# Neighbourhood attention of layer 1: score tiles issued one by one, with the value products of two tiles after every second tile

## The chip, the cores and the metric

The kernel runs on one core of one Trainium2 chip. The metric is the device time of one execution in microseconds (us). The kernel before takes 3551.81 us, the median of 3 runs (3551.78 to 3552.18). One further execution was profiled. Its own time is 3547.52 us, and 3545.7 us lie between its first and its last instruction (the span).

## What is computed

The program has two layers over 2048 latent tokens (a grid of 32 rows by 64 columns) and 256 context tokens, all in float32. The change touches the attention of the second layer ("layer 1") alone. Cut to that:

```python
def one_row(args):                       # one row of 64 queries
    qr, r = args
    r_start = jnp.clip(r - kr // 2, 0, rows - kr)
    kb = lax.dynamic_slice_in_dim(kg, r_start, kr, axis=1)        # 8 rows of keys
    vb = lax.dynamic_slice_in_dim(vg, r_start, kr, axis=1)
    s_lat = jnp.einsum('bqhd,brkhd->bhqrk', qr, kb) * scale + bias
    s_lat = jnp.where(col_mask, s_lat, -jnp.inf)                  # 16 columns of keys
    s_ctx = jnp.einsum('bqhd,bchd->bhqc', qr, k_ctx) * scale
    p = jax.nn.softmax(jnp.concatenate([s_lat, s_ctx], axis=-1), axis=-1)
    return p[..., :kr * GRID_W] @ vb + p[..., kr * GRID_W:] @ v_ctx
...
y = jnp.dot(o * jax.nn.silu(z_x), w_out)
x = x + gate * y
```

There are 16 heads of width 64. Each latent query sees a window of 8 by 16 latent keys and all 256 context keys.

## The kernel before

**Pairs and tiles.** `odd_attention` takes the heads in eight pairs (`j` from 0 to 7). Scores are made transposed: keys on the partitions, queries along the free axis, the two heads of a pair in the two halves of one tile. A *score tile* is 128 keys against all the queries that can see them. A pair has 24 of them: 16 latent ones (l0 to l15, `rect` gives their queries) and 8 context ones (for each of the four blocks of 512 queries, c0 to c3, two halves `u` of the 256 context keys).

**One score tile.** TensorE makes it with eight matmuls on half-arrays (L1785: high times high, low times high, high times low, minus the maximum, each for two heads). It lands in a PSUM buffer `st`; there are two of these, so a tile can begin only when the tile two before it has been read out. ScalarE reads a context tile straight away (`exp`, L108). A latent tile first gets its position bias added by VectorE in one to six pieces (L1961, `st` plus `tab` into `opt`), which is what frees its `st` buffer, and ScalarE then takes `exp` in place.

**Value products.** TensorE multiplies the finished `opt` by the values into PSUM accumulators `o`, one for each block of 512 queries (`tail_ctx` L1797 for context, `tail` L1815 for latent tiles). GpSimd adds the `opt` tiles up into `oacc` (L1821), from which the softmax's denominators come; the two halves of a context block are added first (`sum_ctx`, L1806: c0 and c2 on VectorE, c1 and c3 on GpSimd).

**Ending blocks.** When all tiles of some blocks are done, `finish_blocks` makes the denominators. It is a generator in three parts. The first makes eight matmuls into an `st` buffer (L1840) and a copy on ScalarE; the second takes `Ln`; the third takes `Exp`, then on VectorE L1849 (correction), L1851 (times the gate), L1854 and L1855 (one of each for a block: scale the accumulator, which is then free), and stores the result to `RT1` (L1856). In pairs 0 to 6 the blocks end as [0, 1] and [2, 3], for the last pair as [0], [1] and [2, 3].

**What sets the order.** The order is written out by hand in `steps`: c0 l0 c1 l1 l2 l3 c2 l4 l5 l6 l7 c3 l8 ... l15, twenty steps, where a context step makes both of its tiles. Each step issues its scores, its reading out, then one part of a pending `finish_blocks` (`end`), and puts its value products in the list `pend`. When `pend` holds five steps, `flush(2)` issues the value products of the two oldest; a block that is complete then gets the first part of its ending there. So TensorE sees value products after every second step, and between them two to four score tiles. The loads of the next pair hang on the step number `s` (L1929 to L1941), and on the last pair so do the weights of the output projection (`out_w`, `split` with L1299 on VectorE). The projection of the first 128 tokens (`first`, L131 to L133) begins inside the last pair's steps l14 and l15, in an `o` buffer that block 0 must have given up.

A pool of eleven buffers `opt` holds the tiles that wait for their value products.

Of the kernel before, what the change touches and what calls it, by code (L numbers as in the profile page):

```python
# [12 lines left out]
AF = mybir.ActivationFunctionType  # L13
# [4 lines left out]
P = 128  # L18
# [70 lines left out]
class Kern:  # L89
# [1630 lines left out]
    def odd_attention(self, out, pools, left, wout):  # L1720

        nc = self.nc
        self.RT1 = self.scr("RT1", (KD, P, SEQ), F32)
        NR, NC = (len(b) for b in BLOCKS["k"])
        with ExitStack() as es:
            self.ln_exp(self.last_tanh, es)
            gp, rp, fp, ep, mp, pad, *sets, lp = pools
            pp = self.pool(es, "oaPS", bufs=2, space=PSUM, reuse_waits="tile")
            steps = [("l", n) for n in range(16)]
            for n, at in enumerate((0, 2, 6, 11)):  # L1730
                steps.insert(at, ("c", n))
            both = lambda: self.tl(pp, [P, 2, 512], "st", bufs=2)
            halves = []

# [45 lines left out]
            def scores(ps, ks, qs, j):  # L1780
                terms = [(K[j][0], Q[j][0]), (K[j][1], Q[j][0]), (K[j][0], Q[j][1]), (None, M[j % 2])]
                for n, (k, q) in enumerate(terms):
                    for i in range(2):
                        s = slice(i * 64, i * 64 + 64)
                        mm = nc.tensor.matmul(ps(i), ones[s] if k is None else k[s, ks], qs(q[s]), start=n == 0, stop=n == 3)  # L1785
                return mm
# [2 lines left out]

                return [acc[bb // 2][:, i].rearrange("p r c -> p (r c)")[:, (bb % 2) * 512 : (bb % 2) * 512 + n * 512] for i in range(2)]  # L1790

            def tail_ctx(n, pts, j, V, O, acc):
                O[n] = self.tl(pp, [P, 8, 64], "o", bufs=4)
                o = O[n][:].rearrange("p r c -> p (r c)")
                for u in range(2):
                    for i in range(2):
                        mm = nc.tensor.matmul(o[i * 64 : i * 64 + 64, :], V[:, u, i * 64 : i * 64 + 64], pts[u][:, i, :],  # L1797
                                              start=u == 0, stop=False, skip_group_check=True)
                return mm

            def sum_ctx(n, pts, acc):
# [3 lines left out]
                a = acc[n // 2][:].rearrange("p i r c -> p i (r c)")[:, :, (n % 2) * 512 : (n % 2) * 512 + 512]  # L1805
                (nc.gpsimd if n % 2 else nc.vector).tensor_tensor(out=a, in0=pts[0][:], in1=pts[1][:], op=ALU.add)  # L1806

            def tail(n, pts, j, V, O, acc):
                g, c = divmod(n, 4)
                (r0, nr), (c0, w) = rect("k", g, c)  # L1810
                done = {7: [0], 11: [1], 15: [2, 3]}.get(n, [])
                for bb in range(r0 // 8, (r0 + nr - 1) // 8 + 1):
                    a0, a1 = max(r0, bb * 8), min(r0 + nr, bb * 8 + 8)
                    for i in range(2):
                        mm = nc.tensor.matmul(O[bb][i * 64 : i * 64 + 64, a0 - bb * 8 : a1 - bb * 8, c0 : c0 + w],  # L1815
                                              V[:, NCT + n, i * 64 : i * 64 + 64], pts[:, i, a0 - r0 : a1 - r0, :],
                                              start=False, stop=bb in done, skip_group_check=True)
                for hf in range(r0 // 16, (r0 + nr - 1) // 16 + 1):
                    a0, a1 = max(r0, hf * 16), min(r0 + nr, hf * 16 + 16)
                    a = acc[hf][:, :, a0 - hf * 16 : a1 - hf * 16, c0 : c0 + w]  # L1820
                    nc.gpsimd.tensor_tensor(out=a, in0=a, in1=pts[:, :, a0 - r0 : a1 - r0, :], op=ALU.add)  # L1821
# [65 lines left out]
            Q, K, V, Z, tabs, raw = {}, {}, {}, {}, {}, {}  # L1887
# [9 lines left out]
                fill(K[0], ksrc, CTX + g * 512, CTX + g * 512 + 512)  # L1897
            out_w, out_s = weights(), split()
            pend, late, ends, OA, first_sums = [], [], [], {}, {}
            FIRST_SUMS = {1: 0, 3: 1, 8: 2, 12: 3}  # L1900
            all_k, most, last = slice(0, KD), slice(0, KD - 1), slice(KD - 1, KD)

            def flush(n):

                mm = None
                for f, *a in pend[:n]:
                    mm = f(*a)
                del pend[:n]
                for x in late:
                    x[0] -= 1  # L1910
                for x in [x for x in late if x[0] <= 0]:
                    late.remove(x)
                    ends.append(finish_blocks(*x[1:]))
                    mm = next(ends[-1])
                return mm

            def end(after):
# [4 lines left out]

            for j in range(8):
                OA[j] = {}, {}
                for s, (kind, n) in enumerate(steps):
                    g, c = divmod(n, 4)
                    if s in (1, 10) and j + s > 1:
                        gates(*((j - 1, 1) if s == 1 else (j, 0)))
# [12 lines left out]
                    elif s % 2 and s < 16:  # L1941
                        next(out_w)
                    if kind == "c":
                        pts = []
                        for u in range(2):
                            ps, qs = both(), slice(n * 512, n * 512 + 512)
                            mm = scores(lambda i: ps[:, i, :], slice(u * P, u * P + P), lambda q: q[:, qs], j)
                            pts.append(exps())
                            ex = self.act(pts[u][:], ps[:], AF.Exp)
                        first_sums[n] = pts  # L1950
                    else:
                        (r0_, nr), (c0, w) = rect("k", g, c)
                        a, m, d = even(c0, w)
                        ps, pts = both(), exps()[:, :, : nr * w]
                        pt = pts.rearrange("p i (r c) -> p i r c", r=nr)
                        ps = ps[:, :, : nr * m].rearrange("p i (r c) -> p i r c", r=nr)
                        mm = scores(lambda i: ps[:, i], slice(CTX + n * P, CTX + n * P + P),
                                    lambda q: q.rearrange("d (r c) -> d r c", r=32)[:, r0_ : r0_ + nr, a : a + m], j)
                        for ro, ri, rn in pieces("k", 0, g, r0_, nr):
                            for co, ci, cn in pieces("k", 1, c, c0, w):  # L1960
                                bias = nc.vector.tensor_tensor(out=pt[:, :, ro : ro + rn, co : co + cn],  # L1961
                                                               in0=ps[:, :, ro : ro + rn, d + co : d + co + cn],
                                                               in1=tabs[j][:, :, ri : ri + rn, ci : ci + cn], op=ALU.add)
                        ex = self.act(pts, pts, AF.Exp)
                        pts = pt
                    if s in FIRST_SUMS:
                        with self.tc.issue_after(bias.ins):
                            sum_ctx(FIRST_SUMS[s], first_sums[FIRST_SUMS[s]], OA[j][1])
                    pend.insert(len(pend) - ((kind, n) == ("c", 1)), (tail_ctx if kind == "c" else tail, n, pts, j, V[j], *OA[j]))
# [254 lines left out]
```

## Time and profile before

| what | value |
|---|---|
| median of 3 runs | 3551.81 us |
| profiled execution, its own time | 3547.52 us |
| its span | 3545.7 us |
| mean granted TensorE clock | 0.992 |
| layer 1 attention, first score matmul | at 2962.0 us |
| last pair's first score matmul | at 3302.8 us |
| TensorE busy in the whole span | 3432.9 us (97%) |
| VectorE, ScalarE, GpSimd busy | 2406.5, 1459.8, 1037.6 us |

A row of the timeline gives the start in us, the time until the last of the merged instructions ended, engine, line, operation, the tile written and the tiles read, how many instructions were merged, and in brackets how long the engine had been idle before and what released it. PE is TensorE, PEld its weight loads, DVE VectorE, ACT ScalarE, POOL GpSimd, SP the queue that issues most loads. The count of the value products and of the denominators is twice what the program holds, since each runs as two passes. The granted clock (PEclk) is what share of TensorE's full clock the throttle let through in a stretch.

### The profile page before, as it was taken

The page shows a single profiled execution, that of the slowest core. Times are in us where ns is not written, and L with a number is a line of the kernel's source. Part 1 is how long each engine was busy: PE and PEld are TensorE (multiplying, and loading weights), DVE is VectorE, ACT ScalarE, POOL GpSimd, SP SyncE. Part 2 cuts the span into 40 slices and gives each one's busy share as a digit, 9 for nine tenths or more (in the row PEclk, how much of TensorE's full clock was granted, in tenths as well). Part 3 has the DMA queues.
Part 4 walks back from the last instruction along what each step waited for, and adds up shares of the span by engine and source line. Part 5 has one row for each costly group of instructions (what it writes and reads, how often), then busy time and mean ns, then how long its engine had stood idle before and what let it go on. Part 6 is the DMA issues. An engine that isn't in the chain of part 4 may idle for free.

```text
span 3545.7 us, 54709 instructions
## 1 busy us (share of the span) xinstructions
PE 3432.9 (97%) x20228; PEld 2657.4 (75%) x20228; DVE 2406.5 (68%) x4494; ACT 1459.8 (41%) x2570; POOL 1037.6 (29%) x1281
## 2 busy tenths in 40 slices
PE   8999998999999999999999999999999999988799
PEld 6898987888896666665557878888888886555477
DVE  4677755888886777768876654545678883555765
ACT  5445552111114455446664354445422224555532
POOL 1333431111111333322211133333111114666611
PEclk9999999999999999999999999999999999999999
DMA  7555555233325242334525765445755445554374
GB/s 253 147 157 158 151 142 152 92 109 94 95 73 167 67 130 80 111 112 131 175 80 144 144 197 160 136 129 182 242 151 164 152 139 186 199 200 172 111 191 63
DMA packets 349888, 508.40 MB, mean 143 GB/s; under 512 B 32443, under 2 KB 232843, under 8 KB 342661
## 3 DMA queue, kind: packets, MB, share of 16 engines
q1 hardware_dynamic: 297364, 386.91, 35.9%
q0 software_dynamic: 29232, 82.14, 8.8%
q10 hardware_dynamic: 23024, 35.85, 3.0%
q8 instruction: 160, 2.62, 0.3%
q14 instruction: 108, 0.88, 0.1%
HBM read 325.99 MB, written 196.60 MB: 147 GB/s over the span
## 4 chain that ended last, share of the span: by engine, by line
PE 80%; DVE 6%; DMA 5%; ACT 4%; POOL 3%; issue 3%; SPq 0%; ACTq 0%; DVEq 0%; POOLq 0%
PE st L1175 10%; PE gm L133 10%; PE gm L131 10%; PE gm L132 10%; PE av L1085 7%; PE mx L705 4%; PE st L1785 2%; PE o L1364 2%; PE pu L1364 2%; ACT opt L108 2%; PE st L1364 1%; PE pj L1364 1%; POOL oacc L1821 1%; PE o L1815 1%; PE mx L1697 1%
## 5 line engine op out<-in xcount | busy, mean ns | idle before, releaser
L706 DVE TENSOR_REDUCE mm<-mx 128x1 f32<-128x512 f32 (+1 forms) x656 | 389.1, 627 | 84.3 <-PE mx L705 77.1
L108 ACT ACTIVATE apt<-st 128x1024 f32<-128x1024 f32 (+1 forms) x296 | 300.0, 1014 | 304.4 <-PE st L1175 285.0
L1182 DVE TENSOR_TENSOR acc<-acc,apt 128x1024 f32<-128x1024 f32 x256 | 340.6, 1330 | 83.5 <-ACT apt L108 64.9
L1175 PE MATMUL st<-aq,akh 64*128 64x512 f32 x1728 | 311.8, 408 | 1.1 <-ACT apt L108 0.7
L1085 PE MATMUL av<-apt,av 128*64 128x512 f32 x1152 | 265.8, 598 | 0.0
L1821 POOL TENSOR_TENSOR oacc<-oacc,opt 128x528 f32<-128x528 f32 (+4 forms) x192 | 225.4, 1197 | 75.8 <-ACT opt L108 72.8
L705 PE MATMUL mx<-mk,mq 96*128 96x512 f32 (+1 forms) x656 | 236.0, 373 | 7.5 <-DMA mq<-QC 6.7
L1175 PE MATMUL st<-aq,akl 64*128 64x512 f32 (+1 forms) x1152 | 230.2, 391 | 0.0
L108 ACT ACTIVATE u<-gm 128x352 f32<-128x352 f32 (+1 forms) x140 | 68.6, 496 | 374.7 <-PE gm L133 204.5
L1961 DVE TENSOR_TENSOR opt<-st,tab 128x496 f32<-128x496 f32 (+16 forms) x288 | 123.6, 484 | 137.7 <-PE st L1785 132.2
L1175 PEld LDWEIGHTS st<-aq,akh 64*128 64x128 f32 x1728 | 152.6, 185 | 82.9 <-ACT apt L108 28.5
L1703 DVE CUSTOM_DVE_ANT_1 mx<-mx,mtab 128x105 f32<-128x105 f32 (+14 forms) x576 | 182.9, 339 | 46.9 <-PE mx L1697 35.2
L1085 PEld LDWEIGHTS av<-apt,av 128*64 128x64 f32 x1152 | 76.3, 136 | 135.2 <-issue 133.9
L108 ACT ACTIVATE opt<-opt 128x930 f32<-128x930 f32 (+8 forms) x130 | 104.1, 805 | 137.0 <-DVE opt L1961 116.9
L705 PEld LDWEIGHTS mx<-mk,mq 96*128 96x128 f32 x656 | 121.6, 189 | 19.8 <-issue 7.1
L1175 PEld LDWEIGHTS st<-aq,akl 64*128 64x128 f32 (+1 forms) x1152 | 111.7, 184 | 23.7
L1785 PE MATMUL st<-qh,kh 64*128 64x512 f32 (+6 forms) x384 | 83.0, 427 | 42.4 <-ACT opt L108 24.1
L220 POOL TENSOR_TENSOR oss<-oss,mhalf 128x8 f32<-128x8 f32 x68 | 112.2, 1650 | 5.4
L131 PE MATMUL gm<-w1h,hhi 128*128 128x512 f32 x280 | 111.9, 400 | 0.2 <-ACT ovz L108 0.2
L1552 DVE TENSOR_TENSOR onat<-gm,oss 128x512 f32<-128x512 f32 x68 | 46.8, 689 | 95.6 <-POOL oss L220 95.6
L133 PE MATMUL gm<-w1h,hlo 128*128 128x512 f32 x280 | 110.0, 393 | 0.0
L131 PE MATMUL gm<-w0h,hhi 128*128 128x512 f32 x272 | 109.6, 403 | 0.0
(777 smaller groups left out, 9578.3 us busy)
## 6 DMA issues: line engine op xcount, KB each, us to landing
H<-x ACTq DMA_DIRECT2D x32, 512.0 KB
adaw<-ada_w SPq DMA_DIRECT2D x64, 256.0 KB
wraw<-w_od SPq DMA_DIRECT2D x64, 256.0 KB
K1t<-okt POOLq DMA_DIRECT2D x16, 1024.0 KB, 6.6
x<-H SPq DMA_DIRECT2D x31, 512.0 KB
mtab<-rpb_q SPq DMA_DIRECT2D x16, 899.0 KB
x<-xin SPq DMA_DIRECT2D x18, 512.0 KB
x<-xin POOLq DMA_DIRECT2D x18, 512.0 KB, 5.3
```

The costliest lines, as they stand in the source:

```text
L108: return self.nc.scalar.activation(out, in_, func, **kw)
L131: self.nc.tensor.matmul(out, lh(k), rh(k), start=start and j == 0, stop=False)
L132: self.nc.tensor.matmul(out, lh(k), rl(k), start=False, stop=False)
L133: yield self.nc.tensor.matmul(out, ll(k), rh(k), start=False, stop=stop and j == n - 1)
L705: mm = nc.tensor.matmul(ps[:, :w], q[:A_QK, (t % 6) * P : (t % 6) * P + P], k[:A_QK, k0 : k0 + w], start=True, stop=True)
L706: nc.vector.tensor_reduce(out=m[:, t, n : n + 1], in_=ps[:, :w], axis=AX.X, op=ALU.max)
L1085: mm = nc.tensor.matmul(O[j, nb][i * 64 : i * 64 + 64, :w], V[j, kt // TT][:, kt % TT, i * 64 : i * 64 + 64], pts[:, i, :w], start=n == 0, ...
L1175: mm = nc.tensor.matmul(ps[:, o // 64, :w], k[o : o + r, kb, kq], Q[o : o + r, qb, :w], start=m == 0, stop=m == 4)
L1182: added = nc.vector.tensor_tensor(out=acc[:, :, :w], in0=a[:, :, :w], in1=pts[:, :, :w], op=ALU.add)
L1364: self.mm = self.nc.tensor.matmul(ps, x[:, k, :], y, start=start and k == 0 and n == 0, stop=k == self.H4 - 1 and n == 2, skip_group_check ...
L1703: nc.vector.tensor_tensor_reduce(out=s, in0=s, in1=tb[:, ri : ri + rn, ci : ci + cn], scale=1.0, scalar=-3e38, op0=ALU.add, op1=ALU.max, a ...
L1821: nc.gpsimd.tensor_tensor(out=a, in0=a, in1=pts[:, :, a0 - r0 : a1 - r0, :], op=ALU.add)
```

## The change

The order is now by score tiles: `units` has 24 entries, (kind, n, u), and a context block takes two neighbouring ones. Each unit issues one tile, one part of a pending ending, and puts the value products of that one tile in `pend`; `flush(2)` still comes when `pend` holds five. So two score tiles stand between any two groups of value products. The step numbers on which the sums of context halves hang are moved so that they stay at the same latent tiles (l0, l1, l5, l8). The numbers on which loads hang are kept, so they come after fewer tiles than before. The last pair's ending of block 0 is run through in one go where its first part is issued.

```diff
-            steps = [("l", n) for n in range(16)]
-            for n, at in enumerate((0, 2, 6, 11)):
-                steps.insert(at, ("c", n))
+            units = [("l", n, 0) for n in range(16)]
+            for n, at in enumerate((0, 3, 8, 14)):
+                units[at:at] = [("c", n, u) for u in range(2)]
...
-            def tail_ctx(n, pts, j, V, O, acc):
-                O[n] = self.tl(pp, [P, 8, 64], "o", bufs=4)
+            def tail_ctx(n, pts, j, V, O, acc, u):
+                if u == 0:
+                    O[n] = self.tl(pp, [P, 8, 64], "o", bufs=4)
                 o = O[n][:].rearrange("p r c -> p (r c)")
-                for u in range(2):
-                    for i in range(2):
-                        mm = nc.tensor.matmul(o[i * 64 : i * 64 + 64, :], V[:, u, i * 64 : i * 64 + 64], pts[u][:, i, :],
-                                              start=u == 0, stop=False, skip_group_check=True)
+                for i in range(2):
+                    mm = nc.tensor.matmul(o[i * 64 : i * 64 + 64, :], V[:, u, i * 64 : i * 64 + 64], pts[:, i, :],
+                                          start=u == 0, stop=False, skip_group_check=True)
...
-            FIRST_SUMS = {1: 0, 3: 1, 8: 2, 12: 3}
+            FIRST_SUMS = {2: 0, 5: 1, 11: 2, 16: 3}
...
                     ends.append(finish_blocks(*x[1:]))
                     mm = next(ends[-1])
+                    if x[1] == [0]:
+                        for _ in ends.pop():
+                            pass
...
-                for s, (kind, n) in enumerate(steps):
+                for s, (kind, n, u) in enumerate(units):
...
                     if kind == "c":
-                        pts = []
-                        for u in range(2):
-                            ps, qs = both(), slice(n * 512, n * 512 + 512)
-                            mm = scores(lambda i: ps[:, i, :], slice(u * P, u * P + P), lambda q: q[:, qs], j)
-                            pts.append(exps())
-                            ex = self.act(pts[u][:], ps[:], AF.Exp)
-                        first_sums[n] = pts
+                        ps, pts, qs = both(), exps(), slice(n * 512, n * 512 + 512)
+                        mm = scores(lambda i: ps[:, i, :], slice(u * P, u * P + P), lambda q: q[:, qs], j)
+                        ex = self.act(pts[:], ps[:], AF.Exp)
+                        first_sums[n, u] = pts
...
-                    if j == 7 and 3 < s < 17:
+                    if j == 7 and 3 < s < 20:
```

For TensorE this means at a pair's head: before c0 (two tiles), value products of l12 and l13 of the pair before, l0, c1 (two tiles), value products of l14 and l15, denominators, l1, l2, value products of c0 and c1. Now c0's first tile, value products of l12 and l13, c0's second tile, l0, value products of l14 and l15, denominators, c1 (two tiles), value products of c0, l1, l2, value products of c1, l3, c2's first tile.

VectorE's order moves with it. Its rows at the head of the sixth pair (j = 5) before; `rl` and the first `opt` belong to the ending of blocks 0 and 1 of the pair ahead, and `st_30424` is l0:

```order
L1849 TENSOR_TENSOR rl_30379<-opt_30362,opt_30403 128x1024
L1961 TENSOR_TENSOR opt_30425<-st_30424,tab_30053 128x2x4x8
L1961 TENSOR_TENSOR opt_30425<-st_30424,tab_30053 128x2x4x16
L1961 TENSOR_TENSOR opt_30425<-st_30424,tab_30053 128x2x8x8
L1961 TENSOR_TENSOR opt_30425<-st_30424,tab_30053 128x2x8x16
L1806 TENSOR_TENSOR oacc_5209_30439<-opt_30390,opt_30401 128x2x512
L1851 TENSOR_TENSOR opt_30403<-opt_30403,os_5173_30154 128x1024
L1854 SCALAR_TENSOR_TENSOR o_30043<-rl_30379,o_30043 128x512
L1854 SCALAR_TENSOR_TENSOR o_30048<-rl_30379,o_30048 128x512
```

The same place on VectorE in the changed kernel:

```order
L1849 TENSOR_TENSOR rl_30379<-opt_30362,opt_30392 128x1024
L1851 TENSOR_TENSOR opt_30392<-opt_30392,os_5166_30105 128x1024
L1854 SCALAR_TENSOR_TENSOR o_30016<-rl_30379,o_30016 128x512
L1854 SCALAR_TENSOR_TENSOR o_30053<-rl_30379,o_30053 128x512
L1961 TENSOR_TENSOR opt_30425<-st_30424,tab_30021 128x2x4x8
L1961 TENSOR_TENSOR opt_30425<-st_30424,tab_30021 128x2x4x16
L1961 TENSOR_TENSOR opt_30425<-st_30424,tab_30021 128x2x8x8
L1961 TENSOR_TENSOR opt_30425<-st_30424,tab_30021 128x2x8x16
L1806 TENSOR_TENSOR oacc_5209_30439<-opt_30382,opt_30414 128x2x512
```

Three more rows of the ending (L1851 and both L1854) now stand ahead of l0's bias.

Further on in the same pair, VectorE before, with the ending of blocks 2 and 3 (`rl_30500`); `st_30486` is l1, `st_30506` is l2, `st_30540` is l3:

```order
L1961 TENSOR_TENSOR opt_30487<-st_30486,tab_30053 128x2x124
L1961 TENSOR_TENSOR opt_30487<-st_30486,tab_30053 128x2x248
L1961 TENSOR_TENSOR opt_30507<-st_30506,tab_30053 128x2x124
L1961 TENSOR_TENSOR opt_30507<-st_30506,tab_30053 128x2x248
L1849 TENSOR_TENSOR rl_30500<-opt_30478,opt_30519 128x1024
L1851 TENSOR_TENSOR opt_30519<-opt_30519,os_5206_30422 128x1024
L1854 SCALAR_TENSOR_TENSOR o_30169<-rl_30500,o_30169 128x512
L1854 SCALAR_TENSOR_TENSOR o_30266<-rl_30500,o_30266 128x512
L1961 TENSOR_TENSOR opt_30541<-st_30540,tab_30053 128x2x4x16
```

The same ending (`rl_30475`) and the same three tiles (l1 is `st_30508`, l2 `st_30525`, l3 `st_30543`) on VectorE in the changed kernel:

```order
L1849 TENSOR_TENSOR rl_30475<-opt_30456,opt_30492 128x1024
L1961 TENSOR_TENSOR opt_30509<-st_30508,tab_30021 128x2x124
L1961 TENSOR_TENSOR opt_30509<-st_30508,tab_30021 128x2x248
L1851 TENSOR_TENSOR opt_30492<-opt_30492,os_5204_30411 128x1024
L1854 SCALAR_TENSOR_TENSOR o_30156<-rl_30475,o_30156 128x512
L1854 SCALAR_TENSOR_TENSOR o_30266<-rl_30475,o_30266 128x512
L1961 TENSOR_TENSOR opt_30526<-st_30525,tab_30021 128x2x124
L1961 TENSOR_TENSOR opt_30526<-st_30525,tab_30021 128x2x248
L1855 TENSOR_TENSOR opt_30492<-o_30156,opt_30492 128x512
L1855 TENSOR_TENSOR opt_30492<-o_30266,opt_30492 128x512
L1961 TENSOR_TENSOR opt_30544<-st_30543,tab_30021 128x2x4x16
```

L1849 has moved from behind the biases of l1 and l2 to ahead of both, and L1851 and L1854 stand between the two.

In the last pair, VectorE before at the ending of block 0 (`rl_31777`, accumulator `o_31497`); `st_31840` is l14, `st_31884` l15, L1985 prepares the first projection:

```order
L1849 TENSOR_TENSOR rl_31777<-opt_31760,opt_31796 128x512
L1985 TENSOR_TENSOR opt_31808<-opt_31742,opt_31807 128x896
L1961 TENSOR_TENSOR opt_31841<-st_31840,tab_31023 128x2x248
L1961 TENSOR_TENSOR opt_31841<-st_31840,tab_31023 128x2x93
L1851 TENSOR_TENSOR opt_31796<-opt_31796,os_5388_31622 128x512
L1854 SCALAR_TENSOR_TENSOR o_31497<-rl_31777,o_31497 128x512
L1961 TENSOR_TENSOR opt_31885<-st_31884,tab_31023 128x2x8x17
L1961 TENSOR_TENSOR opt_31885<-st_31884,tab_31023 128x2x8x7
L1961 TENSOR_TENSOR opt_31885<-st_31884,tab_31023 128x2x3x17
L1961 TENSOR_TENSOR opt_31885<-st_31884,tab_31023 128x2x3x7
L1855 TENSOR_TENSOR opt_31796<-o_31497,opt_31796 128x512
```

The same ending (`rl_31737`, `o_31470`) on VectorE in the changed kernel, where `st_31760` is l10 and `st_31781` l11, and L1299 splits weights of the projection:

```order
L1849 TENSOR_TENSOR rl_31737<-opt_31735,opt_31739 128x512
L1961 TENSOR_TENSOR opt_31761<-st_31760,tab_30991 128x2x465
L1851 TENSOR_TENSOR opt_31739<-opt_31739,os_5381_31573 128x512
L1854 SCALAR_TENSOR_TENSOR o_31470<-rl_31737,o_31470 128x512
L1299 TENSOR_TENSOR tab_31638<-opt_31639,tab_31638 128x512
L1855 TENSOR_TENSOR opt_31739<-o_31470,opt_31739 128x512
L1299 TENSOR_TENSOR om_4848_27974<-opt_31685,om_4848_27974 128x512
L1961 TENSOR_TENSOR opt_31782<-st_31781,tab_30991 128x2x15x16
```

The accumulator of block 0 is now read out ahead of l11's bias; before, that came behind l15's.

More of the change, by code (lines that the diff above doesn't have):

```diff
@@ L1806, in sum_ctx, with tail @@
                 (nc.gpsimd if n % 2 else nc.vector).tensor_tensor(out=a, in0=pts[0][:], in1=pts[1][:], op=ALU.add)
-            def tail(n, pts, j, V, O, acc):
+            def tail(n, pts, j, V, O, acc, _):
                 g, c = divmod(n, 4)
@@ L1967, in odd_attention @@
                         with self.tc.issue_after(bias.ins):
-                            sum_ctx(FIRST_SUMS[s], first_sums[FIRST_SUMS[s]], OA[j][1])
-                    pend.insert(len(pend) - ((kind, n) == ("c", 1)), (tail_ctx if kind == "c" else tail, n, pts, j, V[j], *OA[j]))
+                            sum_ctx(FIRST_SUMS[s], [first_sums.pop((FIRST_SUMS[s], u)) for u in range(2)], OA[j][1])
+                    pend.insert(len(pend) - ((kind, n) == ("c", 1)), (tail_ctx if kind == "c" else tail, n, pts, j, V[j], *OA[j], u))
                     end(ex)
-                    if j == 7 and 3 < s < 17:
+                    if j == 7 and 3 < s < 20:
                         with self.tc.issue_after(ex.ins):
```

## The prediction

> **What bounds the kernel now.** I read the page's totals and chain first, then the time of each pair, then one pair's timeline on four engines.
>
> ```profile
> span 3545.7 us, 54709 instructions
> PE 3432.9 (97%) x20228; PEld 2657.4 (75%) x20228; DVE 2406.5 (68%) x4494; ACT 1459.8 (41%) x2570; POOL 1037.6 (29%) x1281
> PE 80%; DVE 6%; DMA 5%; ACT 4%; POOL 3%; issue 3%; SPq 0%; ACTq 0%; DVEq 0%; POOLq 0%
> ```
>
> TensorE carries 80% of the chain; the change deletes no matmul. So it can only change when TensorE waits, how fast it is clocked and how often it restarts. By stretches (us, busy time of PE, PEld, DVE, ACT, POOL, the granted clock), the first pair, two of the middle ones, the last pair, and what follows it:
>
> ```profile
> 2962.00:3003.10 41.10, 39.43 (x362) 25.38 (x362) 18.11 (x36) 20.75 (x24) 32.22 (x27) 1.00 0.68 245
> 3003.10:3053.60 50.50, 45.51 (x402) 28.17 (x402) 28.01 (x52) 26.37 (x30) 32.94 (x29) 0.97 0.49 176
> 3104.10:3153.00 48.90, 43.92 (x402) 27.39 (x402) 28.03 (x52) 26.37 (x30) 33.02 (x29) 1.00 0.50 181
> 3302.80:3363.60 60.80, 47.44 (x400) 29.21 (x400) 47.47 (x66) 35.20 (x49) 38.42 (x28) 0.94 0.37 121
> ```
>
> Pairs two to seven take 48.9 us at full clock and 50.5 at 0.97. No other engine is full, so the waits come from the order of things. TensorE's idle places in the fifth pair (3153.0 to 3203.5), and the one at the next pair's head:
>
> ```profile
> 3160.25 0.50 PE L1785 MATMUL st<-qh,kh 64*128 64x512 f32 x2 [1.96 <-DVE opt L1961]
> 3167.16 0.45 PE L1785 MATMUL st<-qh,kh 64*128 64x384 f32 x2 [0.27 <-ACT opt L108]
> 3174.49 0.50 PE L1785 MATMUL st<-qh,kh 64*128 64x512 f32 x2 [1.12 <-ACT opt L108]
> 3178.54 0.49 PE L1785 MATMUL st<-qh,kh 64*128 64x480 f32 x2 [0.73 <-ACT opt L108]
> 3187.51 0.43 PE L1785 MATMUL st<-qh,kh 64*128 64x360 f32 x2 [0.26 <-ACT opt L108]
> 3203.47 0.50 PE L1785 MATMUL st<-qh,kh 64*128 64x512 f32 x2 [0.52 <-ACT opt L108]
> ```
>
> That is 1.96 + 0.27 + 1.12 + 0.73 + 0.26 + 0.52 = **4.86 us idle in a pair**. Four of the six are a third score tile in a row, or one behind it, waiting for the `st` buffer of the tile two before. Putting value products between them is the right cover for those. The 1.96 is another matter: there a tile waits for l0's bias, which stands on VectorE behind an ending's work.
>
> **What an ending costs VectorE, and GpSimd with it.**
>
> ```profile
> 3167.00 1.00 DVE L1961 TENSOR_TENSOR opt<-st,tab 128x248 f32<-128x248 f32 x2 [2.23 <-PE st L1785]
> 3171.55 1.92 DVE L1849 TENSOR_TENSOR rl<-opt,opt 128x1024 f32<-128x1024 f32 x1 [2.37 <-ACT opt L108]
> 3173.57 1.23 DVE L1851 TENSOR_TENSOR opt<-opt,os 128x1024 f32<-128x1024 f32 x1
> 3174.71 1.29 DVE L1854 SCALAR_TENSOR_TENSOR o<-rl,o 128x512 f32<-128x512 f32 x2
> 3208.52 1.23 DVE L1849 TENSOR_TENSOR rl<-opt,opt 128x1024 f32<-128x1024 f32 x1 [4.51 <-ACT opt L108]
> 3209.66 0.94 DVE L1961 TENSOR_TENSOR opt<-st,tab 128x64 f32<-128x64 f32 x4
> 3162.68 2.36 POOL L1806 TENSOR_TENSOR oacc<-opt,opt 128x1024 f32<-128x1024 f32 x1 [6.93 <-ACT opt L108]
> 3169.05 3.34 POOL L1821 TENSOR_TENSOR oacc<-oacc,opt 128x744 f32<-128x744 f32 x2 [2.02 <-ACT opt L108]
> ```
>
> The same L1849 takes 1.23 with GpSimd idle and 1.92 when it starts at 3171.55 while a GpSimd add runs until 3169.05 + 3.34 = 3172.39: of the 0.84 left to that add it loses 0.69. I read that as VectorE standing still until the add is over, less 0.15.
>
> **The change, part by part.** At each place I put the new order's rows one behind the other with these durations.
>
> *Middle of a pair (l1, l2, l3, c2).* ScalarE and TensorE there:
>
> ```profile
> 3168.82 1.04 ACT L108 ACTIVATE rl<-opt 128x1024 f32<-128x1024 f32 x1
> 3170.48 1.04 ACT L108 ACTIVATE opt<-rl 128x1024 f32<-128x1024 f32 x1
> 3186.44 1.94 ACT L108 ACTIVATE opt<-st 128x1024 f32<-128x1024 f32 x2 [1.37 <-POOL oacc L1821]
> 3182.64 1.94 PE L1797 MATMUL o<-opt,ov 128*64 128x512 f32 x8
> 3175.61 1.34 PE L1815 MATMUL o<-opt,ov 128*64 128x192 f32 x16
> 3200.38 1.89 PE L1840 MATMUL st<-oacc,mtwos 128*64 128x512 f32 x8
> ```
>
> Count from c1's first score matmul. Its tile takes 1.1 (3174.49 to 3175.61 above). ScalarE then runs c1's first `exp`, `Ln`, c1's second `exp`, `Exp`, about 0.94 apart, and is through at 5.1; the ending has moved ahead because `end` is called once a tile. GpSimd's sum of c1 (2.36) starts after the third of these, so L1849, after the fourth, finds about 1.55 of it left: 1.23 + 1.4 = 2.6, until 7.75. l1's bias (1.00) ends at 8.7. TensorE has done c1 (2.2), value products of c0 (1.9), l1 and l2 (1.6), value products of c1 (1.9) by 7.55, and l3 waits for l1's buffer: **1.3 idle**. Then L1851 (1.2) and both L1854 (1.3) stand ahead of l2's bias (1.0), which ends at 12.1; l3 took 0.7, and c2's first tile waits **2.7**. Before, this stretch held 0.27 + 1.12 + 0.73 = 2.1.
>
> *Head of a pair.* L1849 starts about 4.1 after the pair's first score matmul; L1851 and both L1854 now go ahead of l0's bias, so it ends at 4.1 + 1.2 + 1.2 + 1.2 + 0.9 = 8.6. TensorE has two groups of value products, the denominators (1.89) and three score tiles as cover, 7.0 in all: **1.75 idle** where 1.96 was. The 0.52 ahead of c0 stays, and the 0.26 at l8 shrinks to about nothing.
>
> Sum of a pair: 0.52 + 1.75 + 1.3 + 2.7 + 0.05 = 6.3 against 4.86, **+1.4**. Against that go two restarts fewer. A restart is dear:
>
> ```profile
> 3174.82 0.39 PE L1785 MATMUL st<-qh,kl 64*128 64x512 f32 x2
> 3172.28 0.39 PE L1785 MATMUL st<-qh,kh 64*128 64x512 f32 x2
> 3172.52 0.39 PE L1785 MATMUL st<-qh,kl 64*128 64x512 f32 x2
> ```
>
> After a wait or a value product the second term follows the first by 0.33 (3174.49 to 3174.82), in the flow by 0.24 (3172.28 to 3172.52). Two groups of value products more in a pair add two restarts, four waits inside runs of score tiles go: -0.2. Net +1.2 a pair, bounds -2.9 (the waits of 2.38 and the restarts go, nothing comes) and +2.4 (the new waits whole, the 0.52 and 0.26 unchanged and 0.1 for each of four more switches). I take the worked value. Six pairs have an ending at their head: 6 x 1.2 = **+7.2**.
>
> The Trainium skill, "TensorEngine Tiling (Array Packing)", Key Properties, says that changing the tiling mode drains the TensorE, and score tiles and value products use different modes. It speaks against the change; it gives no price, and by the row above four switches more would be +0.4 a pair if no wait inside a run went.
>
> *First pair.* No ending runs in it, so the cover works unopposed. Its small waits go:
>
> ```profile
> 2964.35 0.40 PE L1785 MATMUL st<-qh,kh 64*128 64x288 f32 x2 [0.22 <-ACT opt L108]
> ...
> 2987.14 0.43 PE L1785 MATMUL st<-qh,kh 64*128 64x360 f32 x2 [0.27 <-ACT opt L108]
> ```
>
> Four of 0.2 to 0.35: **-1.0**.
>
> *The clock.* TensorE's clock falls to half in some stretches of 3.41 us:
>
> ```profile
> 3157.86:3161.27 3.41, 1.45 (x12) 0.76 (x8) 3.25 (x7) 1.84 (x3) 0.00 (x0) 1.00 0.00 0
> 3161.27:3164.68 3.41, 3.41 (x22) 2.04 (x22) 3.41 (x5) 1.02 (x1) 2.00 (x1) 0.50 0.35 72
> 3209.06:3212.47 3.41, 1.72 (x16) 1.26 (x18) 3.41 (x7) 1.98 (x3) 0.00 (x0) 1.00 0.00 0
> 3212.47:3215.88 3.41, 3.28 (x26) 1.49 (x22) 2.82 (x6) 1.53 (x2) 2.69 (x2) 1.00 0.55 142
> ```
>
> A stretch in which TensorE was busy 1.45 of 3.41 is followed by one at 0.50; one with 1.72 is not. The 1.96 of idle time does it where it falls whole into one stretch: pairs at 0.97, four of the first seven, 1.6 each (50.5 less 48.9), 6.6 in all. In the new order 1.3 and 2.7 of idle with 0.7 of work between always leave a stretch under 1.5: one in each of six pairs. Each costs about 1.4, since VectorE keeps its pace and the wait behind shrinks: 8.4. Difference **+1.8**.
>
> The Trainium skill, "TensorE: Matmul & The Clock Gate", Part 1, lets the clock fall after an idle window of about 3.4 us, and its table of practice names gaps over 3 us. The trace goes lower: 1.96 idle in 3.41 was enough. By the page, none of my waits (2.7 at most) would halve the clock.
>
> *The last pair.* Its end waits on block 0:
>
> ```profile
> 3369.03 0.80 PE L131 MATMUL o<-wo0h,opt 128*128 128x512 f32 x1 [5.19 <-DVE opt L1855]
> 3363.15 2.38 DVE L1985 TENSOR_TENSOR opt<-opt,opt 128x896 fp32r<-128x896 f32 x1
> 3354.16 1.34 DVE L1299 TENSOR_TENSOR ov<-opt,ov 128x512 fp32r<-128x512 f32 x1 [0.70 <-ACT ov L108]
> ```
>
> With block 0 ended in one go, the projection's buffer is free long before L131, and about 1 of the 5.19 stays (its operand from L1985 and ScalarE's backlog): -4.2. Of the half-clock stretch after it 1.7 go. But its L1849 to L1855 and two L1299 (0.7 to 1.3 each) now stand ahead of l11's bias, and the middle's wait comes too: +1.6. Together **-4.3**, between 0 and -7.
>
> Sum: 7.2 - 1.0 + 1.8 - 4.3 = **+3.7 us**. Against the profiled execution's 3547.5 that gives 3551.2; the median of the runs shown is 4.3 higher, and on it the forecast is 3555.5.
>
> **The rivals.** (A) *The clock decides, slower.* The head's 1.75 idle is just short of the 1.96 that halves the clock. From about 1.9 on, pairs two to seven would have a second half-clock stretch wherever it falls whole into one, and all of L1849's lock makes the middle longer: 6 x 1.6 = 9.6 more, +13 or 3565. For it: GpSimd's adds are late in every pair. Against: half the phases miss. (B) *The cover works, faster.* If the ending's rows come late enough on ScalarE that the biases are not behind them, only 1.96 and 0.52 stay: 6 x (2.38 + 0.5) = 17, less 1.0, 4.3 and some clock: -23, or 3529. Against: VectorE takes its instructions in order. (C) *No lock, or no clock loss.* Without the 1.4 that L1849 loses, or with the page's clock rule, 6 x 1.4 = 8.4 goes: -4.7, or 3547. (D) *Only the end changes*, the pairs come out even: -4, or 3548.
>
> **How the numbers follow.** Forecast 0.50, A 0.24, B 0.12, C and D 0.07 each. A measurement of this kernel can tell about 0.2% (7.1 us) from no change. Slower by more is A and a little of the forecast, 0.25; faster is B, 0.12; within, 0.63. The range leaves out B and the far end of A: 3545 to 3566. The forecast with C and D alone spans 3545 to 3560.
>
> **What would show it.** Right: pairs two to seven at 50.5 to 51.5 us; waits of 1 to 1.5 ahead of l3 and 2.5 to 3 ahead of c2, both on L1961; L1849 at about 2.6 in the middle; a clock of 0.97 in nearly every pair; L131's wait under 2 us. Wrong: L1849 at 1.23 throughout, waits under 4 in a pair, or pairs with two half-clock stretches.

## The result, and the profile after

The changed kernel takes **3557.74 us** in the median of 20 runs (3552.89 to 3567.53), the kernel before 3551.57 (20 runs): a ratio of **1.0020, 95% interval 1.0013 to 1.0027**, +6.2 us by the medians. The forecast was +3.7 us, 3555.5 in 3545 to 3566. It is slower, by about as much as a measurement can just tell from no change.

The page of the changed kernel: its totals and the chain of work that ended last.

```profile
span 3560.7 us, 54719 instructions
PE 3446.4 (97%) x20228; PEld 2671.1 (75%) x20228; DVE 2411.3 (68%) x4494; ACT 1463.3 (41%) x2570; POOL 1041.8 (29%) x1281
PE 80%; DVE 7%; DMA 5%; ACT 3%; issue 2%; POOL 2%; SPq 1%; DVEq 0%; ACTq 0%; POOLq 0%
```

This profiled execution took 3562.45 us and is one of the longer of its 20, and that of before, at 3547.52, one of the shorter of its own. So the first thing to do is to cut the 15.0 us between their spans (3560.7 and 3545.7) by stretch. The stretches of the changed kernel (us, busy time of PE, PEld, DVE, ACT, POOL, granted clock): the first pair, a middle one, the seventh, and all from the last pair to the end of the matmuls.

```profile
2968.84:3008.91 40.07, 39.19 (x360) 25.19 (x360) 17.14 (x35) 20.99 (x24) 30.60 (x27) 1.00 0.69 249
3164.87:3216.50 51.63, 45.26 (x400) 28.66 (x400) 28.66 (x51) 26.43 (x30) 33.95 (x29) 0.97 0.49 172
3267.91:3320.79 52.88, 48.05 (x401) 29.66 (x402) 28.68 (x52) 26.45 (x30) 34.01 (x29) 0.90 0.47 168
3320.79:3555.63 234.84, 216.99 (x1136) 163.30 (x1136) 156.25 (x218) 86.55 (x118) 67.27 (x63) 0.97 0.53 125
```

The same last stretch of the kernel before:

```profile
3302.80:3540.47 237.67, 216.22 (x1136) 163.23 (x1136) 155.41 (x218) 86.36 (x118) 69.88 (x63) 0.97 0.52 123
```

The attention begins at 2968.8 here and at 2962.0 before, although nothing ahead of it was changed: in the nine profiles of this study it begins anywhere from 2962.0 to 2968.8. So 6.8 of the 15.0 is scatter of the stages ahead. What follows is the change, 8.3 in this pair of profiles: the first pair 40.07 for 41.10, **-1.0**; pairs two to seven 3008.91 to 3320.79 for 3003.10 to 3302.80, 311.9 for 299.7, **+12.2**; the last pair and what follows 234.8 for 237.7, **-2.8**. By the runs' interval the change is 4.6 to 9.6 us, and 8.3 lies in it.

TensorE's idle places of the fifth pair (3164.87 to 3216.50), which answer to the six of before:

```profile
3164.87 0.49 PE L1785 MATMUL st<-qh,kh 64*128 64x512 f32 x2 [0.53 <-ACT opt L108]
3173.76 0.50 PE L1785 MATMUL st<-qh,kh 64*128 64x512 f32 x2 [1.79 <-DVE opt L1961]
3182.53 0.40 PE L1785 MATMUL st<-qh,kh 64*128 64x288 f32 x2 [1.30 <-DVE opt L1961]
3186.08 0.79 PE L1785 MATMUL st<-qh,kh 64*128 64x512 f32 x2 [2.77 <-DVE opt L1961]
```

0.53 + 1.79 + 1.30 + 2.77 = 6.39 us in a pair, where 4.86 was. The short waits for ScalarE inside runs of score tiles are gone. Two new waits for a bias on VectorE, 1.30 and 2.77, stand in their place, and the head's wait for l0's bias is 1.79 where it was 1.96. VectorE and GpSimd ahead of the last two:

```profile
3178.92 2.56 DVE L1849 TENSOR_TENSOR rl<-opt,opt 128x1024 f32<-128x1024 f32 x1 [2.97 <-ACT opt L108]
3181.40 0.98 DVE L1961 TENSOR_TENSOR opt<-st,tab 128x248 f32<-128x248 f32 x2
3182.30 1.53 DVE L1851 TENSOR_TENSOR opt<-opt,os 128x1024 f32<-128x1024 f32 x1
3183.76 1.28 DVE L1854 SCALAR_TENSOR_TENSOR o<-rl,o 128x512 f32<-128x512 f32 x2
3184.95 0.98 DVE L1961 TENSOR_TENSOR opt<-st,tab 128x248 f32<-128x248 f32 x2
```
```profile
3178.02 2.37 POOL L1806 TENSOR_TENSOR oacc<-opt,opt 128x1024 f32<-128x1024 f32 x1 [0.99 <-ACT opt L108]
```

L1849, an operation of 1.23 us, is 2.56 long: GpSimd's sum of c1 runs until 3178.02 + 2.37 = 3180.39, and 1.47 of it were left when L1849 started. l1's bias then ends at 3182.38 and l3 starts at 3182.53; L1851 and L1854 go ahead of l2's bias, which ends at 3185.93, and c2's first tile starts at 3186.08.

Stretches of 3.41 us, by their clock:

```profile
3182.72:3186.13 3.41, 0.65 (x10) 0.44 (x8) 3.41 (x6) 0.62 (x2) 1.97 (x2) 1.00 1.03 431
3186.13:3189.54 3.41, 3.41 (x20) 2.35 (x22) 1.84 (x6) 2.08 (x3) 2.12 (x2) 0.50 0.98 407
3015.47:3018.88 3.41, 1.63 (x14) 1.04 (x12) 3.41 (x9) 1.71 (x2) 0.00 (x0) 1.00 0.60 167
3018.88:3022.29 3.41, 3.41 (x24) 1.63 (x22) 1.11 (x2) 3.19 (x4) 0.78 (x2) 1.00 1.00 398
3274.88:3278.29 3.41, 1.63 (x15) 1.42 (x15) 3.41 (x8) 1.92 (x3) 0.00 (x0) 1.00 0.72 195
3278.29:3281.70 3.41, 3.41 (x12) 1.09 (x10) 0.69 (x2) 3.41 (x4) 1.21 (x2) 0.50 1.02 408
3285.12:3288.53 3.41, 1.47 (x12) 0.56 (x8) 3.41 (x6) 0.83 (x1) 2.61 (x2) 1.00 1.03 430
3288.53:3291.94 3.41, 2.83 (x14) 1.91 (x16) 2.47 (x7) 1.54 (x2) 1.91 (x2) 0.50 0.99 414
3291.94:3295.35 3.41, 3.41 (x22) 2.39 (x20) 0.00 (x0) 0.86 (x2) 1.47 (x2) 0.50 1.10 347
```

Each of the six pairs has a half-clock stretch behind its wait ahead of c2 (2.52 in the seventh pair, 2.74 to 2.77 in the others; the first two rows are the fifth pair's). The head's wait of 1.78 is at the edge: in the second pair a stretch with 1.63 us of work is followed by full clock, in the seventh one with 1.63 by half. The seventh pair has three: that one, one after c2's, and a third because the second, at half clock and busy for 2.83 of its 3.41, was not busy enough to end it. In pairs two to seven there are nine such stretches, where before had four.

At the end, the 5.19 us wait ahead of L131 is gone; a 3.91 us wait of a score tile of the last pair is the largest now, behind VectorE's endings and weight splits:

```profile
3378.57 0.66 PE L1785 MATMUL st<-qh,kh 64*128 64x352 f32 x2 [3.91 <-DVE opt L1961]
3384.99 0.50 PE L131 MATMUL o<-wo0h,opt 128*128 128x512 f32 x1
```

### The profile page after: what moved, and what is told of

It reads as the page before. It is cut to its first block, busy times and chain, and to the rows that moved or that the text cites. A ratio compares the mean times of both kernels' runs of the same rounds, so it can differ in the third digit from the quotient of the medians.

```text
span 3560.7 us, 54719 instructions
## 1 busy us (share of the span) xinstructions
PE 3446.4 (97%) x20228; PEld 2671.1 (75%) x20228; DVE 2411.3 (68%) x4494; ACT 1463.3 (41%) x2570; POOL 1041.8 (29%) x1281
## 4 chain that ended last, share of the span: by engine, by line
PE 80%; DVE 7%; DMA 5%; ACT 3%; issue 2%; POOL 2%; SPq 1%; DVEq 0%; ACTq 0%; POOLq 0%
PE gm L133 10%; PE gm L131 10%; PE gm L132 10%; PE st L1175 10%; PE av L1085 7%; PE mx L705 4%; PE st L1785 4%; PE o L1815 2%; PE o L1364 2%; PE pu L1364 2%; PE st L1364 1%; PE pj L1364 1%; PE mx L1697 1%; ACT opt L108 1%; DMA adaw<-ada_w 1%
## 5 line engine op out<-in xcount | busy, mean ns | idle before, releaser
L1175 PE MATMUL st<-aq,akh 64*128 64x512 f32 x1728 | 312.2, 408 | 1.3 <-ACT apt L108 1.0
L1961 DVE TENSOR_TENSOR opt<-st,tab 128x496 f32<-128x496 f32 (+16 forms) x288 | 124.5, 485 | 148.4 <-PE st L1785 148.4
L108 ACT ACTIVATE opt<-opt 128x930 f32<-128x930 f32 (+9 forms) x130 | 104.9, 807 | 147.7 <-DVE opt L1961 140.1
L1785 PEld LDWEIGHTS st<-qh,kh 64*128 64x128 f32 x384 | 38.0, 190 | 110.9 <-issue 73.4
L131 PE MATMUL gm<-w1h,hhi 128*128 128x512 f32 x280 | 111.9, 400 | 0.1
L131 PE MATMUL gm<-w0h,hhi 128*128 128x512 f32 x272 | 110.1, 405 | 0.0
```

The costliest lines, as they stand in the source:

```text
L108: return self.nc.scalar.activation(out, in_, func, **kw)
L131: self.nc.tensor.matmul(out, lh(k), rh(k), start=start and j == 0, stop=False)
L1175: mm = nc.tensor.matmul(ps[:, o // 64, :w], k[o : o + r, kb, kq], Q[o : o + r, qb, :w], start=m == 0, stop=m == 4)
```

## The experiments

Seven kernels were run, four on one chip and then three on another, each in five rounds beside the kernel before (3548.99 us with the first four, 3550.16 with the other three). Ratios are to the kernel before; the changed kernel's own is 1.0020.

**1. One go alone.** The kernel before with the change's last part only:

```
                     mm = next(ends[-1])
+                    if x[1] == [0]:
+                        for _ in ends.pop():
+                            pass
```

> The kernel before, with one part of the change alone: block 0's ending of the last pair runs in one go. My account of the last pair says that this is what took the 5.19 us wait ahead of L131 away and with it the long half-clock stretch there: pairs one to seven as before (41.1, 48.9 or 50.5), the last pair 4 to 7 us shorter, L131 waiting under 1 us; 3545.5 us where before is 3551.5 (-6, between -3 and -8). Rival: the wait went because the change calls end once a score tile, and one go alone does little: 0 to -1, 3551.

Measured: 3545.62 us, ratio 0.9993 (0.9984 to 1.0002). The pairs are as before (41.1, then 48.9 or 50.5). From the last pair on:

```profile
3301.43:3535.43 234.00, 218.01 (x1136) 164.09 (x1136) 156.10 (x218) 86.94 (x118) 70.76 (x63) 0.97 0.53 125
```

That is 3.7 us less than 237.67, just under the 4 to 7 expected, and L131 waits for nothing. The interval of the whole time holds 1, so the gain is seen in this stretch of the profile and not in the time.

**2. Without one go.** The changed kernel, with those three lines taken out.

> The changed kernel without the one-go ending. If the prediction's account of the last pair is whole, the 5.19 us wait ahead of L131 comes back and the kernel is 3 to 6 us slower than the changed one: 3561 to 3564. Rival, which I now hold likelier: with end called once a score tile, block 0's ending is through before L131 asks for its buffer even without the one-go part, so this runs within 1 us of the changed kernel, 3557 to 3559, and one go is one of two ways to the same gain.

Measured: 3558.40 us, ratio 1.0022 (1.0013 to 1.0031), the changed kernel's. From the last pair on:

```profile
3318.76:3552.50 233.74, 217.05 (x1136) 162.55 (x1136) 154.12 (x218) 86.39 (x118) 67.85 (x63) 0.97 0.53 125
```

The gain at the end is there without the one-go ending (233.7 beside 234.8 with it). Either of the two parts brings it; together they bring it once.

**3. The second ending two calls later.** The changed kernel with two calls of `end` left out of each pair. The second ending's `Ln` stays where it was (behind c1's first tile); its third part, `Exp` and all of its rows on VectorE, comes two score tiles later, behind the biases of l1 and l2:

```
-                    end(ex)
+                    if s not in (4, 5):
+                        end(ex)
```

> The changed kernel with end not called at the fourth and fifth score tile of a pair (s of 4 and 5: c1's second tile and l1), so that the second ending of a pair starts two calls later; nothing else. If the ending's rows ahead of the biases of l1 and l2 are what costs (with L1849 held up by GpSimd's sum of c1), then of the waits 0.53 + 1.79 + 1.30 + 2.76 = 6.4 a pair the last two become about 1.5 and 1.1 with value products between them, no stretch of 3.41 us is idle enough to halve the clock, and pairs two to seven take 47.8 to 48.3 us where they took 51.4 to 52.9: 18 to 25 us faster than the changed kernel, 3533 to 3539, and below the kernel before. Rival: value products after every second tile are dear in themselves (restarts, changes between 64-row and 128-row matmuls): then the pairs stay at 50 or more and the time at 3551 or more.

Measured: **3538.35 us, ratio 0.9968 (0.9957 to 0.9980)**. A middle pair, and its idle places:

```profile
3150.11:3198.35 48.24, 43.56 (x400) 27.66 (x400) 28.77 (x51) 26.51 (x30) 35.60 (x29) 1.00 0.51 184
```
```profile
3150.11 0.49 PE L1785 MATMUL st<-qh,kh 64*128 64x512 f32 x2 [0.53 <-ACT opt L108]
3158.99 0.50 PE L1785 MATMUL st<-qh,kh 64*128 64x512 f32 x2 [1.78 <-DVE opt L1961]
3170.75 0.50 PE L1785 MATMUL st<-qh,kh 64*128 64x512 f32 x2 [1.35 <-DVE opt L1961]
3175.96 0.49 PE L1785 MATMUL st<-qh,kh 64*128 64x480 f32 x2 [1.03 <-DVE opt L1961]
```

Pairs two to seven take 48.2 to 48.3 us each, all at full clock. The same order of score tiles and value products, with a part of one ending a little later, is faster than both kernels: by 0.32% than before, and by about 0.5% than the changed one. So value products after every second tile are not dear in themselves.

**4. The wait filled with work.** The changed kernel, l3's scores issued three times:

```
-                        mm = scores(lambda i: ps[:, i], slice(CTX + n * P, CTX + n * P + P),
+                        for _ in range(3 if n == 3 and 0 < j else 1):
+                            mm = scores(lambda i: ps[:, i], slice(CTX + n * P, CTX + n * P + P),
```

> The changed kernel with l3's score matmuls issued three times in pairs two to eight (the repeats compute the same tile again). They add 16 matmuls, about 1.5 us of TensorE time a pair, right in front of c2's first tile, which waits 2.75 us for l2's bias anyway. If TensorE's idle share of a 3.41 us stretch sets its clock, no stretch in the pairs falls under half busy, the clock stays at 1.00 in pairs two to seven, and these take about 50.0 us, although TensorE has more to do: 8 to 12 us faster than the changed kernel, 3546 to 3550. If the half clock comes from something else, the pairs stay at 51.4 to 53 or get longer by part of the 1.5, and the time is 3557 to 3564.

Measured: 3550.97 us, ratio 1.0006 (0.9998 to 1.0015). The fifth and the sixth pair, and the idle places of both (the bias is L1962 here):

```profile
3153.91:3204.18 50.27, 45.00 (x416) 28.56 (x416) 28.61 (x51) 26.43 (x30) 33.96 (x29) 1.00 0.49 176
3204.18:3254.56 50.38, 46.59 (x417) 29.01 (x417) 28.68 (x52) 26.43 (x30) 34.22 (x29) 0.97 0.48 176
```
```profile
3162.79 0.50 PE L1785 MATMUL st<-qh,kh 64*128 64x512 f32 x2 [1.78 <-DVE opt L1962]
3171.55 0.41 PE L1785 MATMUL st<-qh,kh 64*128 64x288 f32 x2 [1.30 <-DVE opt L1962]
3175.09 0.50 PE L1785 MATMUL st<-qh,kh 64*128 64x512 f32 x2 [1.68 <-DVE opt L1962]
...
3213.07 0.50 PE L1785 MATMUL st<-qh,kh 64*128 64x512 f32 x2 [1.78 <-DVE opt L1962]
3225.42 0.50 PE L1785 MATMUL st<-qh,kh 64*128 64x512 f32 x2 [1.47 <-DVE opt L1962]
```

With 16 matmuls more, a pair is 1.3 us shorter than the changed kernel's 51.6. The repeats cost nothing: they take 1.1 us of c2's wait, 2.77 to 1.68. What is saved is the half-clock stretch behind it. So TensorE's idle share does set its clock, and this pair, 50.3 us, is the changed kernel's pair at full clock. The time, 5 us below the changed kernel's by the ratios, is short of the 8 to 12 expected, although in the two profiles these pairs take 9.9 us less; the execution profiled here is the shortest of its 11 (3545.90). My "1.00 in pairs two to seven" missed twice: in the second and sixth pair the head's 1.78 wait halves the clock. There it costs 0.1 us only: the 1.30 ahead of l3 is gone and c2's wait is 1.47 for 1.68, because VectorE went on while TensorE was slow.

**5. GpSimd's sum of c1 taken away.** The changed kernel with

```
+                if n == 1:
+                    nc.gpsimd.memset(a, 512.0)
+                    return
```

> The changed kernel without GpSimd's sum of c1's two tiles: a memset of the same piece takes its place, which waits for no exp (c1's share of the denominators is left out, so the output isn't the reference's). All else, L1849 and its place included, is as changed. If L1849's 2.56 us in the middle of a pair are 1.23 of work and 1.33 of standing still until GpSimd's sum is over, it takes 1.23 here, the 1.29 wait ahead of l3 goes, the wait ahead of c2's first tile stays (2.5 to 2.75), and only part of the pairs still have a half-clock stretch: pairs of 48.7 to 50.4, 7 to 15 us faster than the changed kernel, 3543 to 3551. If the long L1849 has another cause (its exp on ScalarE, its operands), it stays above 2 us, the pairs stay at 51.4 or more and the time at 3557.

Measured: 3542.81 us, ratio 0.9988 (0.9978 to 0.9997). L1849 (L1852 here) in the middle of the fifth pair, two pairs, and the wait that stays:

```profile
3168.82 1.22 DVE L1852 TENSOR_TENSOR rl<-opt,opt 128x1024 f32<-128x1024 f32 x1 [2.96 <-ACT opt L108]
```
```profile
3154.79:3203.08 48.29, 43.55 (x400) 27.60 (x400) 26.99 (x51) 26.42 (x30) 31.22 (x29) 1.00 0.51 184
3203.08:3253.01 49.93, 45.18 (x401) 28.60 (x401) 27.01 (x52) 26.43 (x30) 31.32 (x29) 0.97 0.49 178
```
```profile
3174.33 0.49 PE L1785 MATMUL st<-qh,kh 64*128 64x512 f32 x2 [2.44 <-DVE opt L1964]
```

1.22 for 2.56: the 1.34 between them was standing still behind GpSimd. The 1.30 ahead of l3 goes with it, and three of six pairs have no half-clock stretch. Pairs of 48.3 to 49.9 and 3542.81 are just below the 48.7 to 50.4 and 3543 to 3551 expected.

**6. Endings early, old grouping.** The kernel before with `end` called after each of a context step's two tiles, and one go:

```
                             ex = self.act(pts[u][:], ps[:], AF.Exp)
+                            if u == 0:
+                                end(ex)
```

> The change without its regrouping: the kernel before, whose score tiles and value products keep their order, with end called after each score tile (24 times a pair) and block 0's ending in one go. If endings that come earlier are what costs, whatever the grouping, pairs two to seven rise to 51 or more and the time to 3558 to 3565. If it takes both (the ending's rows ahead of l1's and l2's biases, and score tiles that come two at a time and ask for their buffers then), the waits here are spread in pieces under 1.5 us, no stretch is idle enough to halve the clock, pairs take 49.2 to 50 us each, and with the last pair's 4 us the time is 2 to 6 us below the kernel before: 3545 to 3549. I hold the second.

Measured: 3553.42 us, ratio 1.0012 (1.0003 to 1.0020), between the two expectations: mine failed. Pair two (3006.72 to 3056.82) at full clock, pair five, and those larger idle places of pair two that the kernel before does not have:

```profile
3006.72:3056.82 50.10, 43.95 (x400) 27.26 (x400) 29.16 (x51) 26.21 (x30) 33.92 (x29) 1.00 0.49 177
3157.97:3209.64 51.67, 45.51 (x400) 28.08 (x400) 28.95 (x51) 26.20 (x30) 33.69 (x29) 0.97 0.48 172
```
```profile
3011.79 0.50 PE L1785 MATMUL st<-qh,kh 64*128 64x512 f32 x2 [1.05 <-ACT opt L108]
3014.16 0.50 PE L1785 MATMUL st<-qh,kh 64*128 64x512 f32 x2 [1.18 <-ACT opt L108]
3030.25 0.43 PE L1785 MATMUL st<-qh,kh 64*128 64x360 f32 x2 [1.01 <-DVE opt L1966]
```

At full clock the pair (pair two is the only one) is 50.1, and 48.9 with the old calls: more calls of `end` cost 1.2 us a pair in the old grouping too. They do it in another way, though. The second ending's VectorE rows still stand behind the biases of l1 and l2, as before. The 1.05 and 1.18, 2.23 together, are waits for ScalarE at the head where 1.96 for l0's bias was. The 1.01 is a wait for l3's bias: L1851 ahead of it starts at 3025.69 and takes 2.48 for 1.23, since GpSimd's adds run until 3027.08 here. GpSimd's sum of c1 comes behind the store of the first ending, 12.2 us into the pair, where it started 9.7 into it before (3162.68 in the pair from 3152.97).

And the clock did fall, in five of six pairs: two waits close together, here 1.01 and 0.75, empty a stretch as one long wait does:

```profile
3180.22:3183.63 3.41, 1.65 (x18) 1.09 (x16) 3.29 (x9) 1.60 (x3) 1.29 (x2) 1.00 1.00 388
3183.63:3187.04 3.41, 3.41 (x24) 2.05 (x20) 2.23 (x2) 1.76 (x2) 1.78 (x2) 0.50 1.19 313
```

**7. The second ending one call later.** The changed kernel with one call left out of each pair, the first of the two of run 3:

```
-                    end(ex)
+                    if s != 4:
+                        end(ex)
```

> The changed kernel with one call of end left out (at c1's second tile, s of 4), half of what the run with two calls left out did. If the place of the second ending is the cause, one step later already takes it past l1's bias: the 1.29 wait ahead of l3 goes, one wait of 2.2 to 2.5 stays at c2's first tile, and the difference to the run with two calls is mostly the clock: a wait over 1.9 in one piece halves it in some pairs. Pairs of 48.2 to 48.6 without and about 50 with a half-clock stretch, two to four of six with one; 8 to 12 us below the kernel before: 3538 to 3543. If the gain of the run with two calls left out came from fewer calls as such, this one gives half of it, 3546.

Measured: 3542.65 us, ratio 0.9982 (0.9971 to 0.9992). The fourth and the fifth pair, and their largest waits:

```profile
3103.02:3151.09 48.07, 43.61 (x401) 27.40 (x402) 28.34 (x52) 26.28 (x30) 34.63 (x29) 1.00 0.51 184
3151.09:3203.99 52.90, 47.84 (x401) 29.82 (x402) 29.01 (x52) 26.27 (x30) 33.80 (x29) 0.90 0.47 168
```
```profile
3125.60 0.44 PE L1785 MATMUL st<-qh,kh 64*128 64x360 f32 x2 [2.15 <-DVE opt L1961]
...
3175.86 0.67 PE L1785 MATMUL st<-qh,kh 64*128 64x360 f32 x2 [2.75 <-DVE opt L1961]
```

Without a half-clock stretch the pair is even a little shorter than in 3 (48.07 for 48.24), so the place of the ending, not the number of calls, is what counts. The wait that stays, 2.15, is ahead of l4 and not ahead of c2's first tile, where I had expected it. Four of six pairs have half-clock stretches. Two have one, and take 49.5 to 49.6; two have three, and take 52.9 where I had expected about 50.

## Why the prediction was right, point by point

The mechanism was right: endings that come earlier on VectorE, the standing still behind GpSimd, and the clock behind the longer waits. Each of the three large terms was too good, by 1.2, 2.0 and 1.5 us, and no error offset another. That the time stayed in the range owes something to its width, 21 us for a change of 3.7: the 8.3 of the profiles is about half-way to rival A's 13.

Of the signs named for being right, the waits (1.30 and 2.77, both on L1961), L1849's 2.56 and L131 came true. Pairs at 50.5 to 51.5 did not: one of six lies there (51.41), the others take 51.6 to 52.9. The clock is 0.97 in four of six, 0.94 and 0.90 in the other two. And one sign named for being wrong came true: two pairs have two or three half-clock stretches. So part of rival A happened.

- **The pair, forecast +1.2 at full clock, measured +1.4.** A pair of the changed kernel takes 50.3 at full clock (run 4, whose repeats lie inside a wait) and one of before 48.9: 6 x 1.4 = 8.4 for 7.2. The waits forecast were 0.52, 1.75, 1.3, 2.7; measured 0.53, 1.79, 1.30, 2.77. The 0.26 at l8 went, as expected. What I set against them for fewer restarts, 0.2, was nearer to 0.1 (waits +1.53, pair +1.4).
- **The lock behind GpSimd, forecast 1.4 of L1849's 2.6.** L1849 measures 2.56, and run 5 takes 1.34 of it away by taking GpSimd's sum away. Where VectorE's rows move, other ones meet GpSimd's adds: L1851 takes 2.48 in run 6 (above). The Trainium skill, "SBUF — State Buffer", Who interferes with whom, says that a VectorE instruction with two SBUF inputs contends with a GpSimd instruction that reads SBUF. The rows agree, and give the price here.
- **The cause, endings ahead of biases.** Run 3 moves only the third part of the second ending and takes 2.0 us out of a pair at full clock (48.24 for 50.27); run 7, one call later, takes 2.2. With the ending there the new order is 0.7 better than before (48.24 for 48.9). So the +1.4 is 2.0 for the second ending's place less 0.7 for the rest of the change. How much of the 0.7 is the grouping alone isn't shown, since run 3 keeps the other calls of `end`. Rival B's mechanism exists in part, 0.7 at full clock of the 2.9 it named, and the change as made does not reach it. Run 6 is no second proof of this cause, since its 1.2 comes by other waits; but that both grouping and endings are needed for a loss, as I held ahead of it, is not so.
- **The clock, forecast +1.8, measured about +3.8: mis-sized.** Pairs two to seven take 311.9, of which 6 x 50.3 = 301.8 at full clock: 10.1 from the clock; before, 299.7 less 6 x 48.9 is 6.3 (the forecast has 6.6, though its own 4 x 1.6 is 6.4). Runs 1 and 2, whose pairs two to seven are those of the two kernels, take 298.1 and 312.2, so the difference varies with the execution. I counted one stretch a pair; there are nine in six pairs, at 1.1 each and not 1.4. Two are second stretches that follow a slow one which the wait ahead of c2 still reaches into. One follows the head's 1.78 wait, which is rival A; A's price of 1.6 each was too high, since the waits behind take most of it up (run 4: 0.1). The Trainium skill, "TensorE: Matmul & The Clock Gate", Part 1, has the clock fall after an idle window of about 3.4 us. By that rule none of these pairs, with waits of 2.77 at most, would have slowed, and filling a wait, as run 4 does, would not have made a pair shorter.
- **The last pair, forecast -4.3, measured -2.8: mis-sized, and given to the wrong part.** The step "with block 0 ended in one go" named a sufficient cause (run 1: -3.7), but in the changed kernel the more frequent calls of `end` do it already (run 2). TensorE's idle time there falls by 3.6 (237.67 less 216.22 for 234.84 less 216.99): the whole 5.19 ahead of L131, where I took off 4.2, less a net 1.6 of other waits, the 3.91 among them, which is what I had set against it. The term that failed is the clock. I took off 1.7 for a half-clock stretch, but both kernels spend 13.7 us of this part at half clock (two stretches in a row twice: from 3325.1 and 3366.1 before, from 3343.1 and 3377.3 now), and TensorE's busy time rises by 0.8.
- **The first pair, forecast -1.0, measured -1.0.**

Sum: 8.4 - 1.0 + 3.8 - 2.8 = 8.4, by the profiles 8.3, for 3.7; by the medians 6.2. (The upper bound given for a pair, +2.4, comes to 2.1 by the terms it names.) The bound of 0.2% runs through the measured interval, so "within" and "slower" can't be told apart. Not tried: the new grouping with all of `end`'s old calls, 20 a pair.

## What to carry to other kernels

When the order of work on the bounding engine is changed, write down what else moves by it: here a helper that is called once a step ran 24 times instead of 20, and its rows in front of the biases cost 2.0 us a pair where the rest of the change gave 0.7. Work that has to be done some time is best put where the engine that does it has nothing due; two calls later turned a loss of 0.2% into a gain of 0.3%. A wait is also a clock matter: count the idle time of a whole 3.41 us stretch, not the longest gap, and ask whether a wait behind takes the slow stretch up.

## What the runs showed of the hardware that was not expected

- TensorE's clock fell after stretches of 3.41 us with 1.45 (before) or 1.65 us (run 6) of work in them and not after one with 1.72 (before); of two with 1.63 (changed) it fell after one. The busy time that the trace shows gives no sharp limit: in run 6 the clock fell after 1.76 (from 3111.95) and 1.99 (from 3361.12) too. Two waits of 1.01 and 0.75 did it (run 6) as one of 1.96 did (before).
- A half-clock stretch busy for 2.83 of 3.41 was followed by another (changed, seventh pair); one busy for 3.04 (sixth pair) and those busy throughout were followed by full clock.
- A half-clock stretch of 3.41 us cost from 0.1 us (run 4, sixth pair, waits behind it) to 1.6 us (run 5, 49.93 for 48.29, none behind).
